# First attention of a two-layer trunk: banks of PSUM given out by use, and TensorE's order written down

## The chip, the cores and the metric

The kernel runs on one core of a Trainium2 chip. The metric is device time in microseconds (us) of one execution. Before the change the median of three runs is 1443.74 us (1443.34 to 1444.59).

## What is computed

A trunk of two layers over 1024 latent tokens (16 rows of 64) and 256 context tokens, model width 1024, 16 heads of 64. Cut to what matters:

```python
u, uc = h * (1 + scale) + shift, hc * (1 + scale_c) + shift_c   # adaLN, per layer
# layer 0, mixer_a: windowed attention, 4 key heads, a sink logit for each head
q, k, v, g = split(u @ w_in);  q, k = apply_axial_rope(q), apply_axial_rope(k)
qc, kc, vc, gc = split(uc @ w_in)
# each block of 128 queries: its own block of keys, one on each side, and the context
p = softmax(concat([mask(q @ k.T), q @ kc.T, sink]))
y = ((p_lat @ v + p_ctx @ vc) * silu(g)) @ w_out     # context queries: context keys only
h = layer_norm(ALPHA * h + gate * y);  hc likewise
# layer 1, mixer_b: 2-D neighbourhood attention with a relative bias, the same frame
```

## The kernel before

Everything is computed as fp32 in two parts, a rounded high part and the rest (`hi`, `lo`), so a product is three matmuls (hi x hi, hi x lo, lo x hi). A program of this size is written with a tile framework: code asks pools for tiles, and a scheduler gives each engine its own list of instructions, in an order that follows from priorities and its own cost estimates. `lift(n)` raises the priority of what stands in it. `keep_in_program_order(ins)` ties an instruction behind the one of its engine that the code issued just before it.

**The stages.** Keys and values of layer 0 are projected first (until 81 us). Then comes the *first attention*, until about 601 us: eight pairs of heads `p`, ten blocks of 128 queries `b` (eight of latents, two of context), two heads `h`; that makes 160 units `A0` to `A159`, twenty a pair. Out-projection and layer norm of layer 0 follow, then layer 1.

**One unit of attention.** Its steps are `S_A` (scores, 256 to 640 keys, matmuls in `qkA`), `m_A` (DVE: scale, mask and minimum out of PSUM into `s`, `sm_first`), the exponential (ACT) with its sum, `rs_A` (DVE), the division (POOL), `T_A` (TensorE transposes of `s` into PSUM, `sm_transpose`), then `pth_A` (ACT: high part of T) and `ptl_A` (DVE: the low part), and for two heads together the value product `pvA` with the high part first and the low part later. `otmp` (ACT and DVE) takes `pvA` out of PSUM.

**Projections between attention.** While pair p is in attention, the g of pair p and the q of pair p+1 are projected: for each, three chunks of tokens (512, 512, 256) named `pj<weights>_<chunk>`, eight pieces of three matmuls a chunk. `merge` weaves the list of attention pieces with the list of projection pieces by their costs. A chunk of q is rotated when it is done (`rope_evac`: shuffle L470 into `rb`, multiply L471 into `ra`, L472 on POOL, add L473), then split into `qA` (L660 on ACT, L661 on DVE). `ra` and `rb` have one buffer each; the third chunk, of context tokens, isn't rotated and goes straight from PSUM into `qA`. A chunk of g goes through `th` (tanh, also in tag `ra`). `gj` and `gw` are dot products for the layer's gate, in between.

**PSUM.** Eight banks: two pairs of banks (`psbig`), which S and T share in turn with whatever else needs a pair, and four single banks (`psone`) for projections and values.

Of the kernel before, what the change touches and what calls it, by code (L numbers as in the profile page):

```python
# [33 lines left out]

AHEAD_A, LIFT_A = 3, 80
AHEAD_B, LIFT_B = 3, 40
BARE_B = 108

GATED_LAST = 1 << 20
# [42 lines left out]

def build(tc, i, out):
    nc = tc.nc
    mm = nc.tensor.matmul
    dma = nc.sync.dma_start
    es = ExitStack()

# [3 lines left out]
        return p, st  # L92

    dr = es.enter_context(tc.tile_pool(name="dr", bufs=1, space=DRAM))
    ps = es.enter_context(tc.tile_pool(name="ps", bufs=1, space=PSUM))

    def psbig(name):
        return ps.tile([P, 1024], F32, tag="big", bufs=2, name=name)

    def psone(name):  # L100
        return ps.tile([P, 512], F32, tag="one", bufs=4, name=name)
# [88 lines left out]
    def proj_pieces(j0, u, chunks, evac):  # L190

        pieces = []
        state = {}

        def piece(ci, t0, n, kq):
            def run():
                if ci == 0 and kq == 0:
                    w.split(j0 + 2)
                    w.split(j0 + 4)
                    w.load(j0 + 6)  # L200
                if kq == 0:
                    state["ps"] = psone(f"pj{j0}_{ci}")
                pt = state["ps"]
                for kt in (kq,):
                    hi, lo = w.got[j0 + kt // 4]
                    sl = slice((kt % 4) * P, (kt % 4 + 1) * P)
                    rh, rl = u.at(kt, slice(t0, t0 + n))
                    mm(pt[:, :n], hi[:, sl], rh, start=kt == 0, stop=False)  # L208
                    mm(pt[:, :n], hi[:, sl], rl, start=False, stop=False)  # L209
                    mm(pt[:, :n], lo[:, sl], rh, start=False, stop=kt == KT - 1)  # L210
# [59 lines left out]

        return evac

    def g_evac(pl, g):


        def evac(pt, t0, n):
            th = pl.tile([P, 512], F32, tag="ra", bufs=1, name="th")
            nc.scalar.activation(th[:, :n], pt[:, :n], AF.Tanh, scale=0.5)
            nc.vector.scalar_tensor_tensor(
                g[:, t0 : t0 + n], th[:, :n], 1.0, pt[:, :n], ALU.add, ALU.mult  # L280
            )

        return evac

    def merge(att, fill, lead=0.0):

        ta = sum(a[0] for a in att) or 1.0
        tf = sum(f[0] for f in fill)
        ia = jf = 0
        ca = cf = 0.0  # L290
# [41 lines left out]
    def sm_transpose(s, order, pt, hl, name):  # L332

        n = len(order)
        tp = psbig(f"T_{name}")
        for k, src in enumerate(order):
            nc.tensor.transpose(tp[:, k * P : (k + 1) * P], s.t[:, src * P : (src + 1) * P], ident)  # L337
        tv = tp[:, : n * P].rearrange("p (k q) -> p k q", k=n)
        a = name[0] == "A"
        with lift(20 if a else 0):  # L340
            nc.scalar.copy(pt.hi[:, :n, hl, :], tv)  # L341
        with lift(60 if a else 0):
            nc.vector.tensor_tensor(pt.lo[:, :n, hl, :], tv, f32(pt.hi[:, :n, hl, :]), ALU.subtract)  # L343
# [116 lines left out]
    adc = pp.tile([P, KT, 2, 2], F32, name="adc")  # L460


    def rope_evac(store, pl, bufs):
        def evac(pt, t0, n):
            if t0 >= S:
                store(pt[:, :n], t0, n)
                return
            a = pl.tile([P, 512], F32, tag="ra", bufs=bufs, name="ra")
            b = pl.tile([P, 512], F32, tag="rb", bufs=bufs, name="rb")
            nc.vector.stream_shuffle(b, pt, SWAP)  # L470
            nc.vector.tensor_tensor(a, pt, cos[:, t0 : t0 + n], ALU.mult)  # L471
            nc.gpsimd.tensor_tensor(b, b, sin[:, t0 : t0 + n], ALU.mult)  # L472
            nc.vector.tensor_tensor(a, a, b, ALU.add)  # L473
            store(a, t0, n)

        return evac
# [125 lines left out]
    def dot_half(h, j):  # L602
        def run():
            dot_sum()
            if j == 0:
                gh.clear()
                for v in range(2):
                    t = px.tile([P, 512], F32, tag=f"gh{v}", bufs=1, name="gh")
                    dma(t, bass.AP(i["cr"].tensor, v * D + h * 512, [[0, P], [1, 512]]))
                    th = px.tile([P, 512], F32, tag="gw", bufs=2, name="gth")  # L610
                    nc.scalar.activation(th, t, AF.Tanh, scale=0.5)
                    nc.vector.scalar_tensor_tensor(t, th, 1.0, t, ALU.add, ALU.mult)
                    gh.append(t)
# [3 lines left out]
            o = ap_.tile([P, 512], F32, tag="ra", bufs=1, name="gj")  # L617
            nc.vector.tensor_tensor_reduce(o, t, gh[0], 0.5, 0.0, ALU.mult, ALU.add, accum_out=acc[:, j, 0:1])
            nc.gpsimd.tensor_tensor(t, t, gh[1], ALU.mult)
            sums.append((t, acc[:, j, 1:2]))  # L620

        return (0.0, run, 0)
# [22 lines left out]
    pp_st.close()  # L645
    pq, pq_st = pool("attA", "right")


    qA, gA, kA, vA = {}, {}, {}, {}

# [12 lines left out]
        return store  # L663

    def qprojA(p):
        return proj_pieces(pos["Aq", p], uA, CHUNKS, rope_evac(q_store(p), ap_, 1))

    def gprojA(p):
        def gev(pt, t0, n):
            if t0 == 0:  # L670
                gA[p] = pq.tile([P, T], F32, tag="gA", bufs=2, name=f"gA{p}")
            g_evac(ap_, gA[p])(pt, t0, n)

        return proj_pieces(pos["Ag", p], uA, CHUNKS, gev)

# [77 lines left out]
    def att_steps(subs, qk, st, tr, pv, last_of_unit, costs, need, ahead, rise, split=False):  # L753
# [3 lines left out]
        for k in range(-ahead, n + 2 + split):  # L757
            row = []

            def t_piece(k=k):  # L760
                if k + 1 < n:
                    with lift(rise(k)):
                        sm_second(st[k + 1])
                if k >= 0:
                    tr(k)

            def s_piece(k=k):
                qk(k + ahead)

            def v_piece(k=k):  # L770
                pv(k - 2)

            def v_first(k=k):
                pv(k - 2, 0)

            def v_second(k=k):
                pv(k - 3, 1)

            if -1 <= k < n:
# [28 lines left out]
    v_loadA(0)  # L808
    merge([], qprojA(0))
    px, px_st = pool("attA2", "right")  # L810
    for p in range(8):
        att = [x for row in rowsA[p * 20 : (p + 1) * 20] for x in row]
        if p % 2 == 0 and p:
            k_load(p // 2, 1)
        if p % 2 == 1 and p < 7:
# [9 lines left out]
        else:  # L825
# [10 lines left out]

            def og_first():
                oA0.extend(og_small(og_load(0, 0)))
                yA0.extend(psone(f"yA0_{nh}") for nh in range(2))

            fill.append((0.0, og_first))
            for n in range(2 * KT):
# [4 lines left out]
                gate_rows(gts[:, v], dcol[:, 0:8, v])  # L847
            raw = og_load(0, 1)
            merge(att[-6:], [])
    px_st.close()  # L850
    pq_st.close()
    ap_st.close()
# [39 lines left out]
    for b in range(10):  # L892
# [24 lines left out]
        if b < 8:  # L917
            dma(zdd[b * P : (b + 1) * P, :], z)
        pend = (b, z)

    def k_evac(dst, pl):
        def evac(pt, t0, n):
# [285 lines left out]
    for b in range(8):  # L1208
# [31 lines left out]
        for sl in parts:  # L1240
            nc.vector.scalar_tensor_tensor(z[:, sl], z[:, sl], rs[:, 1:2], vecs[3][:, sl], ALU.mult, ALU.add)  # L1241
            dma(grid_rows(out, b)[:, :, sl], z[:, sl])
    ob_st.close()
    ub_st.close()
    wp_st.close()
# [94 lines left out]
```

## Time and profile before

| | before |
|---|---|
| median of three runs | 1443.74 us (1443.34 to 1444.59) |
| the profiled execution | 1443.36 us |
| its span in the profile | 1441.6 us |
| granted TensorE clock, mean | 0.994 |
| busy: PE, DVE, ACT, POOL | 97%, 68%, 51%, 44% |

The span runs from the first to the last instruction that the profiler saw; about 1.8 us lie around it. A line of a group gives code line, engine, operation, output and input, shapes and count, then the busy time, the mean ns of one and the idle time of the engine just ahead of it with what ended that. In the timeline the bracket at the end gives the idle time ahead of an instruction and its releaser.

### The profile page before, as it was taken

To read this page: it belongs to the slowest core of one execution; us is meant where nothing else is said; L and a number is where in the kernel's file an instruction comes from. 1 tells how busy PE (TensorE), PEld (TensorE's weight loads), DVE (VectorE), ACT (ScalarE), POOL (GpSimd) and SP (SyncE) were. 2 spreads that over 40 slices of the span, in tenths; PEclk is the share of its full clock that TensorE was granted. 3 is DMA by queue.
4 is the path that set the end of the run, shared out by engine and by line. 5 is a ranking of instruction groups with operands and counts; after the bars stand their busy time and mean duration, and the time that the engine had idled before them with its cause. 6 is when DMAs were issued, how large, how long until landed. Compare 5 with 4: busy or idle time off the path is not lost. (4 is left out here: it accounts for less than half of the span.)

```text
span 1441.6 us, 25151 instructions
## 1 busy us (share of the span) xinstructions
PE 1392.6 (97%) x8816; PEld 1215.4 (84%) x8816; DVE 987.3 (68%) x2216; ACT 733.6 (51%) x1561; POOL 630.8 (44%) x779
## 2 busy tenths in 40 slices
PE   9999999999999999999999999999999999998995
PEld 5887888888888888788898899888988899887775
DVE  4658888878888789566433765555565565667698
ACT  4336776677676778333222545544454444557310
POOL 0326766666666657233211333333233323336664
PEclk9999999999999999999999999999999999999998
DMA  9472114123122114433287565564555565384353
GB/s 367 171 234 81 53 59 132 46 78 97 66 78 63 56 61 128 128 132 132 74 256 217 160 192 159 140 166 145 170 150 156 144 179 146 103 208 145 115 133 93
DMA packets 117229, 195.05 MB, mean 135 GB/s; under 512 B 9328, under 2 KB 57840, under 8 KB 117104
## 3 DMA queue, kind: packets, MB, share of 16 engines
q1 hardware_dynamic: 117104, 193.45, 44.5%
q8 instruction: 70, 1.15, 0.3%
q14 instruction: 55, 0.45, 0.1%
HBM read 141.51 MB, written 51.90 MB: 134 GB/s over the span
## 5 line engine op out<-in xcount | busy, mean ns | idle before, releaser
L330 POOL TENSOR_SCALAR s_B<-s_B,rs_B 128x640 f32<-128x640 f32 (+1 forms) x128 | 101.9, 797 | 292.0 <-DVE rs_B L329 250.9
L208 PE MATMUL pj<-uBh,wh 128*128 128x512 f32 (+1 forms) x448 | 175.9, 393 | 0.0
L209 PE MATMUL pj<-uBl,wh 128*128 128x512 f32 (+1 forms) x448 | 170.2, 380 | 0.0
L210 PE MATMUL pj<-uBh,wl 128*128 128x512 f32 (+1 forms) x448 | 170.0, 379 | 0.0
L325 ACT ACTIVATE s_B<-s_B,m_B 128x640 f32<-128x640 f32 (+1 forms) x128 | 102.9, 804 | 127.9 <-DVE m_B L318 127.7
L325 ACT ACTIVATE s_A<-s_A,m_A 128x641 f32<-128x641 f32 (+2 forms) x160 | 119.5, 747 | 88.5 <-DVE m_A L318 73.5
L164 POOL TENSOR_TENSOR wl<-wr,wh 128x512 fp32r<-128x512 f32 x64 | 87.7, 1371 | 157.8 <-ACT wh L162 135.4
L330 POOL TENSOR_SCALAR s_A<-s_A,rs_A 128x640 f32<-128x640 f32 (+2 forms) x160 | 127.1, 794 | 58.5 <-DVE rs_A L329 56.3
L318 DVE CUSTOM_DVE_ANT_0 s_A<-S_A,msk,nsk 128x640 f32<-128x640 f32 (+2 forms) x160 | 123.6, 774 | 34.0 <-PE S_A L706 17.7
L343 DVE TENSOR_TENSOR pt_B<-T_B,pt_B 128x640 fp32r<-128x640 f32 (+1 forms) x128 | 101.0, 789 | 63.4 <-ACT pt_B L341 62.9
L208 PE MATMUL pj<-uAh,wh 128*128 128x512 f32 (+1 forms) x384 | 139.9, 364 | 0.0
L209 PE MATMUL pj<-uAl,wh 128*128 128x512 f32 (+1 forms) x384 | 137.6, 358 | 0.0
L210 PE MATMUL pj<-uAh,wl 128*128 128x512 f32 (+1 forms) x384 | 137.3, 357 | 0.0
L343 DVE TENSOR_TENSOR ptl_A<-T_A,pth_A 128x640 fp32r<-128x640 f32 (+2 forms) x160 | 114.0, 713 | 15.3 <-PE pvA L734 7.1
L337 PE MATMUL T_A<-ident,s_A 128*128 128x128 f32 x672 | 101.0, 275 | 12.1 <-DVE m_A L318 8.6
L337 PEld LDWEIGHTS T_A<-ident,s_A 128*128 128x128 f32 x672 | 77.2, 140 | 40.2 <-issue 16.6
L341 ACT CAST pt_B<-T_B 128x640 fp32r<-128x640 f32 (+1 forms) x128 | 84.4, 659 | 47.8 <-PE T_B L337 47.4
L318 DVE CUSTOM_DVE_ANT_0 s_B<-S_B,bias 128x640 f32<-128x640 f32 (+1 forms) x128 | 100.5, 785 | 10.6 <-PE S_B L1037 9.6
L341 ACT CAST pth_A<-T_A 128x640 fp32r<-128x640 f32 (+2 forms) x160 | 96.5, 603 | 16.7 <-PE T_A L337 14.0
L210 PEld LDWEIGHTS pj<-uBh,wl 128*128 128x128 f32 x448 | 84.3, 188 | 16.7
L337 PE MATMUL T_B<-ident,s_B 128*128 128x128 f32 x608 | 88.3, 274 | 6.0 <-POOL gB L1078 2.3
L209 PEld LDWEIGHTS pj<-uBl,wh 128*128 128x128 f32 x448 | 84.7, 189 | 9.1
(219 smaller groups left out, 3885.3 us busy)
## 6 DMA issues: line engine op xcount, KB each, us to landing
kB<-kdB SPq DMA_DIRECT2D x64, 320.0 KB, 5.3
gw<-in_wadaT SPq DMA_DIRECT2D x48, 256.0 KB, 2.8
vdB<-st SPq DMA_DIRECT2D x20, 512.0 KB, 3.4
vB<-vdB SPq DMA_DIRECT2D x16, 640.0 KB, 4.8
wada<-in_wadaC SPq DMA_DIRECT2D x16, 512.0 KB, 9.7
kdB<-st SPq DMA_DIRECT2D x16, 512.0 KB, 2.9
qdB<-st SPq DMA_DIRECT2D x16, 512.0 KB, 3.5
qB<-qdB SPq DMA_DIRECT2D x32, 256.0 KB, 4.6
```

The costliest lines, as they stand in the source:

```text
L164: e.tensor_tensor(lo, r, f32(hi), ALU.subtract)
L208: mm(pt[:, :n], hi[:, sl], rh, start=kt == 0, stop=False)
L209: mm(pt[:, :n], hi[:, sl], rl, start=False, stop=False)
L210: mm(pt[:, :n], lo[:, sl], rh, start=False, stop=kt == KT - 1)
L318: nc.vector.tensor_tensor_reduce(outp, sc, in1, scale, init if init is not None else 3e38, ALU.add, ALU.min, accum_out=s.m)
L325: nc.scalar.activation(s.t[:, :n], s.t[:, :n], AF.Exp, bias=s.m, scale=-1.0, accum_out=s.sum)
L330: nc.gpsimd.tensor_scalar(s.t[:, : s.w], s.t[:, : s.w], s.rs, 1.0, ALU.mult, ALU.mult)
L337: nc.tensor.transpose(tp[:, k * P : (k + 1) * P], s.t[:, src * P : (src + 1) * P], ident)
L341: nc.scalar.copy(pt.hi[:, :n, hl, :], tv)
L343: nc.vector.tensor_tensor(pt.lo[:, :n, hl, :], tv, f32(pt.hi[:, :n, hl, :]), ALU.subtract)
```

## The change

1. **Banks by use.** From the end of the key and value projections to the end of the first out-projection block, the pool is a new one: S has one pair of banks, T two pairs in turn, projections one bank (`pj`), value products one bank (`pv`). Before and after that stretch there are pools as before; in the last the pairs take strict turns.
2. **A copy out of the projection bank.** Each chunk of q and g is copied by ACT (L505 of the changed kernel for q, into `ra`; for g into `gA`), with a lift of 40. Shuffle and multiply, tanh and gate then read that copy; the rotation works in `ra` itself. `gj` moves from tag `ra` to `rb`.
3. **A gap behind each chunk.** `merge` holds projection pieces back for 1700 cost units of attention after a chunk's last piece. The hold starts at zero in each call, that is in each pair, and lapses when the attention list is used up.
4. **Values in twos of units.** The value products of an even block are issued high and low part together.
5. **TensorE's order as the code writes it**, for pairs 0 to 6 (`pin`); the eighth pair is left to the scheduler. At the start of every second pair the first three score pieces are moved back by a row or so.

```diff
+LIFT_PJ = 40
+GAP_PJ = 1700.0
...
-    mm = nc.tensor.matmul
+    pinned = []
+    def pin(ins):
+        if pinned:
+            tc.keep_in_program_order(ins)
+    def mm(*a, **kw):
+        pin(nc.tensor.matmul(*a, **kw))
...
+        def big(self, name):
+            use = name[0] if name[0] in self.tags else "S"
+            t = self.tags[use]
+            n = self.n[use] = self.n.get(use, -1) + 1
+            return self.ps.tile([P, 1024], F32, tag=f"big{t[n % len(t)]}", bufs=1, name=name)
+        def one(self, name):
+            if self.ones == 4:
+                return self.ps.tile([P, 512], F32, tag="one", bufs=4, name=name)
+            return self.ps.tile([P, 512], F32, tag=name[:2], bufs=1, name=name)
...
+    banks.st.close()
+    banks.open("psA", {"S": (0,), "T": (1, 2)}, 2)
...
-            return (3 * 0.425 * n, run)
+            return (3 * 0.425 * n, run, GAP_PJ) if kq == 7 and j0 < NA else (3 * 0.425 * n, run)
...
-            if jf < len(fill) and (ia == len(att) or jf < need or cf - lead <= ca * (tf - lead) / ta):
+            if jf < len(fill) and (ia == len(att) or jf < need or (ca >= hold and cf - lead <= ca * (tf - lead) / ta)):
                 cf += fill[jf][0]
                 fill[jf][1]()
+                if len(fill[jf]) > 2:
+                    hold = ca + fill[jf][2]
...
-    def rope_evac(store, pl, bufs):
+    def rope_evac(store, pl, bufs, free=False):
         def evac(pt, t0, n):
+            if t0 < S or free:
+                a = pl.tile([P, 512], F32, tag="ra", bufs=bufs, name="ra")
+            if free:
+                with lift(LIFT_PJ):
+                    nc.scalar.copy(a[:, :n], pt[:, :n])
+                pt = a
...
             if split and 0 <= k - 2 < n and last_of_unit(k - 2):
-                row.append((costs[2] / 2, v_first, 0))
+                if subs[k - 2][1] % 2:
+                    row.append((costs[2] / 2, v_first, 0))
             elif split and k - 3 >= 0 and last_of_unit(k - 3):
-                row.append((costs[2] / 2, v_second, need(k - 3, k + ahead)))
+                if subs[k - 3][1] % 2:
+                    row.append((costs[2] / 2, v_second, need(k - 3, k + ahead)))
+                else:
+                    row.append((costs[2], v_both, need(k - 3, k + ahead)))
...
+        if p == 7:
+            pinned.clear()
+        elif p % 2 == 0 and p:
+            s = [rows_p[n].pop(1) for n in range(3)]
+            rows_p[1].append(s[0])
+            rows_p[2].insert(1, s[1])
+            rows_p[2].append(s[2])
```

**Between two pairs.** TensorE before, at the boundary of pairs 1 and 2 (`pj16_2` is the last chunk of the next pair's q, `pj18_0` the first of that pair's g):

```order
L208 MATMUL pj16_2_2604<-uAh2_107,wh17_1873 128x256
L209 MATMUL pj16_2_2604<-uAl2_110,wh17_1873 128x256
L210 MATMUL pj16_2_2604<-uAh2_107,wl17_1874 128x256
L208 MATMUL pj18_0_2697<-uAh0_105,wh18_2269 128x512
L209 MATMUL pj18_0_2697<-uAl0_108,wh18_2269 128x512
L210 MATMUL pj18_0_2697<-uAh0_105,wl18_2270 128x512
L337 MATMUL T_A37_2703<-ident_63,s_A37_2573 128x128 x2
L705 MATMUL S_A40_2708<-kA1_0_2126,qA4_2426 128x256
```

The same place on TensorE now, where both chunks have the one projection bank:

```order
L96 MATMUL pj16_2_2652<-uAh2_107,wh17_1888 128x256
L96 MATMUL pj16_2_2652<-uAl2_110,wh17_1888 128x256
L96 MATMUL pj16_2_2652<-uAh2_107,wl17_1889 128x256
L96 MATMUL pj18_0_2719<-uAh0_105,wh18_2333 128x512
L96 MATMUL pj18_0_2719<-uAl0_108,wh18_2333 128x512
L96 MATMUL pj18_0_2719<-uAh0_105,wl18_2334 128x512
L372 MATMUL T_A37_2725<-ident_63,s_A37_2586 128x128 x2
```

The chunks still follow each other directly; S_A40 has moved further back. ACT before, at the same place:

```order
L660 CAST qA4_2426<-ra_2583 64x512
L660 CAST qA5_2427<-ra_2583 64x512
L743 COPY otmp_2598<-pvA1_4_2478 64x256
L341 CAST pth_A36_2647<-T_A36_2649 128x2x128
L325 ACTIVATE s_A39_2660,sum_A39_2662<-s_A39_2660,m_A39_2661 128x257
L660 CAST qA4_2426<-pj16_2_2604 64x256
L162 CAST wh21_2689<-wr21_2279 128x512
L341 CAST pth_A36_2647<-T_A37_2703 128x2x128
L660 CAST qA5_2427<-pj16_2_2604 64x256
```

And ACT now; `ra_2596` is the copy of q's second chunk, `ra_2698` that of the third, in the same buffer:

```order
L704 CAST qA4_2445<-ra_2596 64x512
L704 CAST qA5_2446<-ra_2596 64x512
L641 ACTIVATE gw_2485,dcol_71<-gw_2485 128x512
L376 CAST pth_A36_2645<-T_A36_2647 128x2x128
L190 CAST wh21_2711<-wr21_2343 128x512
L505 COPY ra_2698<-pj16_2_2652 128x256
L704 CAST qA4_2445<-ra_2698 64x256
L704 CAST qA5_2446<-ra_2698 64x256
```

The copy of the third chunk stands behind the cast `wh21`; both casts into `qA` come after it.

**At S_A41 and S_A42**, the second and third units of pair 2. TensorE before:

```order
L705 MATMUL S_A41_2745<-kA1_1_2682,qA5_2427 128x256
L706 MATMUL S_A41_2745<-kA1_1_2682,qA5_2427 128x256
L208 MATMUL pj18_0_2697<-uAh0_105,wh19_2273 128x512
L209 MATMUL pj18_0_2697<-uAl0_108,wh19_2273 128x512
L210 MATMUL pj18_0_2697<-uAh0_105,wl19_2274 128x512
L337 MATMUL T_A39_2775<-ident_63,s_A39_2660 128x128 x2
L734 MATMUL pvA1_8_2795<-pth_A36_2647,vA0_981 128x256 x2
L208 MATMUL pj18_0_2697<-uAh0_105,wh19_2273 128x512
L705 MATMUL S_A42_2780<-kA1_0_2126,qA4_2426 128x384
```

TensorE now:

```order
L372 MATMUL T_A39_2782<-ident_63,s_A39_2671 128x128 x2
L96 MATMUL pj18_0_2719<-uAh0_105,wh19_2337 128x512
L96 MATMUL pj18_0_2719<-uAl0_108,wh19_2337 128x512
L96 MATMUL pj18_0_2719<-uAh0_105,wl19_2338 128x512
L96 MATMUL S_A41_2790<-kA1_0_2157,qA5_2446 128x256 x2
L96 MATMUL S_A41_2790<-kA1_1_2704,qA5_2446 128x256 x2
L96 MATMUL S_A42_2802<-kA1_0_2157,qA4_2445 128x384
L96 MATMUL S_A42_2802<-kA1_0_2157,qA4_2445 128x256
```

S_A42 now stands directly behind S_A41, in the one pair of banks that scores have.

**At the start of the first attention.** ACT before, from the evacuation of the last value projection (`pv-1_4`) on:

```order
L266 ACTIVATE st_902<-pv-1_3_853 128x4x64 x2
L266 ACTIVATE st_965<-pv-1_4_908 128x4x64 x2
L660 CAST qA0_1030<-ra_1024 64x512
L660 CAST qA1_1031<-ra_1024 64x512
L162 CAST wh12_1103<-wr12_995 128x512
L162 CAST wh13_1107<-wr13_997 128x512
L660 CAST qA0_1030<-pj8_2_1071 64x256
```

ACT now, where `pj8_0`, `pj8_1` and `pj8_2` are the chunks of the first q:

```order
L294 ACTIVATE st_902<-pv-1_3_853 128x4x64 x2
L294 ACTIVATE st_965<-pv-1_4_908 128x4x64 x2
L505 COPY ra_1028<-pj8_0_1003 128x512
L704 CAST qA0_1035<-ra_1028 64x512
L704 CAST qA1_1036<-ra_1028 64x512
L505 COPY ra_1066<-pj8_1_1041 128x512
L190 CAST wh12_1111<-wr12_999 128x512
```

The copies are new; the first stands behind the evacuation of `pv-1_4`.

More of the change, by code (lines that the diff above doesn't have):

```diff
@@ L94, in build, with open @@
     dr = es.enter_context(tc.tile_pool(name="dr", bufs=1, space=DRAM))
[L95 to L101, printed above, removed]
+    class Banks:
+        def open(self, name, tags, ones):
+            self.st = ExitStack()
+            self.ps = self.st.enter_context(tc.tile_pool(name=name, bufs=1, space=PSUM, reuse_waits="tile"))
+            self.tags, self.ones, self.n = tags, ones, {}
+        def big(self, name):
[7 more added lines that the diff above has]
+            return self.ps.tile([P, 512], F32, tag=name[:2], bufs=1, name=name)
+    banks = Banks()
+    banks.open("ps0", {"S": (0, 1)}, 4)
+    psbig, psone = banks.big, banks.one
     cp = es.enter_context(tc.tile_pool(name="cp", bufs=1, side="left"))
@@ L838, in og_first @@
                 oA0.extend(og_small(og_load(0, 0)))
-                yA0.extend(psone(f"yA0_{nh}") for nh in range(2))
+                banks.tags["T"] = (1,)
+                y = banks.ps.tile([P, 1024], F32, tag="big2", bufs=1, name="yA0")
+                yA0.extend(y[:, sl] for sl in HALVES)
             fill.append((0.0, og_first))
@@ L919, in build @@
         pend = (b, z)
+        if b == 0:
+            banks.st.close()
+            banks.open("psB", {"S": (0, 1)}, 4)
     def k_evac(dst, pl):
```

26 lines of the change are left out of this document (18 added, 8 removed).

## The prediction

> **What bounds the kernel now.** I read the page's engine lines first, then the stretches, then TensorE's waits in the first attention, then single stretches of the timeline.
>
> ```profile
> span 1441.6 us, 25151 instructions
> PE 1392.6 (97%) x8816; PEld 1215.4 (84%) x8816; DVE 987.3 (68%) x2216; ACT 733.6 (51%) x1561; POOL 630.8 (44%) x779
> ```
>
> PE is busy for 97% of the span, so time can come only from PE's idle time. The change touches nothing outside the first attention that PE would notice. That stretch, 81 to 601 us, has these rows, one for each pair of heads after the start (us, then busy of PE, weight load, DVE, ACT, POOL, clock, DMA):
>
> ```profile
> core 0: us, PE busy (x) PEld busy (x) DVE busy (x) ACT busy (x) POOL busy (x), PEclk, DMA share, GB/s
> 98.20:158.70 60.50, 55.00 (x354) 47.63 (x353) 48.46 (x116) 39.94 (x91) 38.04 (x54) 1.00 0.35 98
> 158.70:218.70 60.00, 58.77 (x385) 51.70 (x385) 49.41 (x122) 42.79 (x98) 40.24 (x58) 1.00 0.20 66
> 218.70:280.40 61.70, 59.34 (x384) 51.69 (x384) 50.63 (x122) 42.43 (x98) 40.45 (x57) 1.00 0.29 89
> 280.40:341.40 61.00, 59.05 (x384) 51.88 (x384) 50.47 (x123) 43.37 (x100) 40.36 (x59) 1.00 0.21 69
> 341.40:403.20 61.80, 59.35 (x384) 51.74 (x384) 50.70 (x122) 42.51 (x98) 40.36 (x57) 1.00 0.30 90
> 403.20:462.90 59.70, 58.50 (x384) 51.79 (x384) 49.06 (x121) 42.50 (x98) 40.25 (x59) 1.00 0.20 62
> 462.90:523.60 60.70, 60.23 (x391) 52.87 (x391) 48.40 (x121) 41.46 (x94) 36.86 (x55) 1.00 0.21 67
> 523.60:601.50 77.90, 71.20 (x439) 61.06 (x438) 61.62 (x138) 52.87 (x113) 42.59 (x61) 1.00 0.36 111
> ```
>
> A pair takes some 60 us at the full granted clock, and PE stands still for 0.5 to 2.5 of it (5.5 and 6.7 in the first and the last; 21.9 us in all eight). DVE is at 80% there, ACT at 70%: they are not the bound, but anything that waits for them waits behind a queue. The waits of PE between 98 and 580 us:
>
> ```profile
> PE T_A L337 <- DVE m_A L318: 8.6, 14, 1.6
> PE S_A L705 <- DVE ptl_A L343: 5.1, 7, 1.2
> PE S_A L706 <- DVE ptl_A L343: 1.8, 6, 0.3
> PE T_A L337 <- POOL gw L619: 1.3, 1, 1.3
> PE T_A L337 <- DVE rs_A L329: 0.5, 1, 0.5
> ```
>
> The first three are waits for a pair of banks: scores S and transposes T take turns in the same two pairs, so a T waits until the first softmax step (`m`, L318) has emptied a later unit's scores, and an S waits until `ptl` has emptied a T. Together 15.5 us in 27 waits: what the new division of banks can give back by name.
>
> **What the change gives.** T gets two pairs of its own; between a T and the `ptl` that frees its pair lie now some 5 us of PE work at the median (3.0 before), counted from the order with the PE prices below. These waits go: -15.5 us. S has one pair alone: S(k+1) may start when `m` of S(k) has run, and nothing else.
>
> **What S waits for now.** The price of one such step, from a place where DVE was prompt:
>
> ```profile
> 212.56 0.41 PE L706 MATMUL S_A<-kA,qA 128*128 128x256 f32 x2
> 213.12 0.48 DVE L318 CUSTOM_DVE_ANT_0 s_A<-S_A,msk,nsk 128x256 f32<-128x256 f32 x1
> 217.35 0.08 DVE L318 DVE_READ_ACCUMULATOR2_ANT m_A<- 128x1 f32 x1
> 217.58 0.41 PE L337 MATMUL T_A<-ident,s_A 128*128 128x128 f32 x2 [0.16 <-DVE m_A L318]
> L318 DVE CUSTOM_DVE_ANT_0 s_A<-S_A,msk,nsk 128x640 f32<-128x640 f32 x96 | 84.6, 881 | 25.8 <-POOL s_A L330 11.7 <-PE S_A L706 11.7 <-POOL s_A L323 1.8
> L318 DVE CUSTOM_DVE_ANT_0 s_A<-S_A,msk,nsk 128x512 f32<-128x512 f32 x32 | 23.7, 749 | 6.2 <-PE S_A L706 5.6
> 111.27 0.74 PE L337 MATMUL T_A<-ident,s_A 128*128 128x128 f32 x5 [0.26 <-DVE m_A L318]
> 111.78 0.44 PE L705 MATMUL S_A<-kA,qA 128*128 128x384 f32 x1
> ```
>
> S ends at 212.97, DVE starts 0.15 later; `m` ends at 217.43 and PE starts 0.15 later; so from the end of one S to the next S it takes 0.15 + 0.88 + 0.08 + 0.15 = 1.26 us for 640 keys, 1.13 for 512, 0.86 for 256. In the new order PE has 1.93 us of other work between at the median, which covers it. It doesn't at 23 of 159 places. At S_A1, S_A42, S_A82, S_A122 and S_A157 nothing lies between (the order at S_A42 is shown); at S_A7 and at the six of S_A31 to S_A131 only five transposes, by the last two rows 0.51 us. Five at 0.86 to 1.13, seven at 0.72, the other eleven together 2.8: 13.2 us. The same arithmetic on before's `T_A <- m_A`, with distances from its order, gives 6.6 us where the trace has 8.6, so it errs low; half of 13.2 (several fall behind a stall in which DVE catches up) to 17.2 (13.2 x 8.6 / 6.6) are the ends. I take 13.2, the plain sum.
>
> **What one projection bank costs at the start.** Before, the three chunks of the first q follow each other without a gap, in three banks. Now each waits for the ACT copy of the one ahead, and in ACT's order the first copy stands behind the evacuation of the value projections:
>
> ```profile
> 86.51 0.39 PE L210 MATMUL pj<-uAh,wl 128*128 128x512 f32 x1
> 86.73 0.39 PE L208 MATMUL pj<-uAh,wh 128*128 128x512 f32 x1
> 90.45 0.39 ACT L266 ACTIVATE st<-pv-1_4_908 128x256 fp32r<-128x256 f32 x1 [0.49 <-DVE st L267]
> 92.17 0.28 PE L208 MATMUL pj<-uAh,wh 128*128 128x256 f32 x1
> L278 ACT ACTIVATE th<-pj 128x512 f32<-128x512 f32 x16 | 9.6, 599 | 2.3 <-PE pj L210 2.1
> L472 POOL TENSOR_TENSOR rb<-rb,sin 128x512 f32<-128x512 f32 x14 | 18.0, 1288 | 10.4 <-DVE rb L470 10.4
> L473 DVE TENSOR_TENSOR ra<-ra,rb 128x512 f32<-128x512 f32 x14 | 10.5, 748 | 0.8 <-POOL rb L472 0.7
> L660 ACT CAST qA<-ra 64x512 fp32r<-64x512 f32 x29 | 17.9, 618 | 5.8 <-DVE ra L473 5.4
> ```
>
> Chunk 0 is done at 86.73 (the row there is the next chunk's first). ACT reaches the copy at 90.84; with 0.60 for 128x512 out of PSUM (L278) and the hand-off PE starts chunk 1 at 91.5: 4.75 us lost. Chunk 1 takes 5.44 (86.73 to 92.17), its copy 0.75: 0.75 lost. Chunk 2 takes 2.9, but its copy goes into the same `ra`, the only one, in which chunk 1's rotation runs: shuffle 0.75 (the row of 211.10 below), POOL 1.29, add 0.75, two casts 1.24, last subtract 0.69, five hand-offs of 0.1, then the 256-wide copy 0.37: 5.6 + 0.15, against 2.9, so 2.85 lost. Start: 8.35 us, between 7.0 and 9.5 as the hand-offs are none or double and DVE is late by a piece.
>
> **What it costs between pairs.** GAP_PJ keeps attention work behind each chunk, but the hold starts from zero in each pair's merge: chunk 2 of q is followed at once by chunk 0 of the next g (the order at this place is shown), in the one bank. Before, the same place, between pairs 1 and 2:
>
> ```profile
> 210.59 0.40 PE L210 MATMUL pj<-uAh,wl 128*128 128x512 f32 x1
> 211.10 0.75 DVE L470 STREAM_SHUFFLE rb<-pj 128x512 f32<-128x512 f32 x1
> 215.55 1.36 DVE L661 TENSOR_TENSOR qA<-ra,qA 64x512 fp32r<-64x512 f32 x1 [0.32 <-ACT qA L660]
> 217.47 0.69 DVE L661 TENSOR_TENSOR qA<-ra,qA 64x512 fp32r<-64x512 f32 x1
> 216.45 0.28 PE L210 MATMUL pj<-uAh,wl 128*128 128x256 f32 x1
> 216.57 0.40 PE L208 MATMUL pj<-uAh,wh 128*128 128x512 f32 x1
> 218.31 0.62 ACT L162 CAST wh<-wr 128x512 fp32r<-128x512 f32 x1
> 218.67 0.39 PE L705 MATMUL S_A<-kA,qA 128*128 128x256 f32 x1 [0.68 <-DVE ptl_A L343]
> ```
>
> Chunk 1 of q is done at 210.82, its rotation leaves `ra` at 218.16, 7.34 us later, since DVE does attention work in between; chunk 2 is done at 216.57, 5.75 us after chunk 1. Now chunk 1's copy (0.60) goes ahead of the shuffle, and chunk 2's copy waits for `ra`: 7.34 + 0.60 + 0.05 + 0.37 + 0.15 = 8.5 us after chunk 1, where PE is ready at 5.75: 2.75 us. Five boundaries have this distance; the first has 5.14 (3.35 lost), the last 6.89 (1.6 lost): 18.7 us over seven. Low end: `ra` is free by then; but the copy stands on ACT behind the cast `wh` of L162, which reuses weights that chunk 2 reads last (the row of 218.31: it ran after chunk 2), so 0.62 + 0.37 + 0.2 = 1.2 us stay at six, 7.5 in all. High end: the sixteen DVE instructions that the new order puts from the shuffle on to the last subtract have 7.2 us of work and start 1.5 us after chunk 1, `ra` free at 9.2: 27.5. I take 18.7, nearest to the measured row.
>
> **The other parts.** 48 copies of 0.37 to 0.6 us are 26 us of ACT work, 3 us a pair, in ACT's 30% of free time: nothing on the path but where the bank is waited for, above. The g chunks and q's first find at least 1.48 us of PE work behind them, over twice a copy; nothing. Shuffle and multiply read SBUF instead of PSUM: L473 does so already at 748 ns, no gain. `gj` in `rb` rather than `ra`: nothing. Values in twos: the same matmuls, their bank is written again at least 3 us after its last matmul (1.1 at one place, at the end); nothing. Transposes and score matmuls keep their count, as do DVE, POOL and SP; no DMA moves past another. Layer B runs as before but for 176 of 3955 matmuls that change places among themselves: nothing. Each wait also drains PE: a 128x256 matmul lasts 0.28 and the next starts 0.12 later (216.45 to 216.57), so 0.16 a wait; 33 waits for 27: +1.0.
>
> [...]
>
> **Sum.** -15.5 + 13.2 + 8.35 + 18.7 + 1.0 = +25.8 us. The profiled execution took 1443.4 (span 1441.6 and 1.8 around it), the median is 1443.7: 1469 us. Its own range: 7.5 + 7.0 + 6.6 - 15.5 = +5.6, or 27.5 + 9.5 + 17.2 + 1.0 - 15.5 = +39.7: 1449 to 1483.
>
> **Rivals.**
> *Faster: one stall absorbs the others.* If PE stands at a boundary, DVE and ACT catch up, and the S waits, which need DVE late or a bare distance, fall into time already lost; only floors remain, 7.5 at boundaries and 7.0 at the start. Against it the gain is 15.5, the further 1.8 us of waits in the rows above and up to 4.6 us, the rest of the 21.9: -7.4, 1436. It decides where all new waits together stay under 16 us. For it: the waits before are few and short (27 of 320 units). Against: S_A1, S_A42, S_A82, S_A122 lie bare in the order, and the start's 4.75 us are independent of DVE.
> *No change: boundaries at the floor, S as reckoned at its low half.* 7.5 + 8.35 + 6.6 - 15.5 - 1.8 - 4.6: about 0, 1441 to 1447.
> *Much slower: every group waits.* If ACT is behind by a cast or two when a chunk ends (0.62 each, and 70% busy), a distance of 1.48 to 2.3 us doesn't cover the copy, and some 38 more groups wait 0.4 each: +15 beyond the sum, 1484 or more. Against: the copy's lift of 40 puts it ahead of most in ACT's order.
>
> **Chances.** The forecast 0.68, every group waits 0.09, no change 0.10, faster 0.13. A measurement here tells 0.2%, 2.9 us, from no change. Of the forecast's own mass a little lies above 1483, of the faster case about half below 1439; the range is 1440 to 1484. Faster 0.13, within 0.2% 0.10, slower 0.77.
>
> **What would show it.** In the profile after: `T_A <- m_A` and `S_A <- ptl_A` gone; instead `pj <- ACT ra` with seven waits of 1 to 4 us at the boundaries and three at the start, one over 4 us; `S_A <- m_A` with some 23 waits and 13 us. The stretch from 81 us to the first S longer by 8 us; a middle pair 61 to 64 us. Wrong it would be if ACT's first copy isn't held by the value evacuations, if the rotation leaves `ra` within 6 us, or if pairs get shorter by more than their named waits.

## The result: slower by 5.3%, three times what was forecast

| | before | after |
|---|---|---|
| median | 1444.16 us | 1520.82 us |
| ratio, 95% interval | | 1.053 [1.049, 1.056] |
| profiled execution | 1443.36 us | 1525.82 us (the longest of four; the others 1518.5 to 1521.0) |

The first lines of the page after:

```profile
span 1524.0 us, 25148 instructions
PE 1424.3 (93%) x8815; PEld 1244.7 (82%) x8816; DVE 994.0 (65%) x2216; ACT 758.2 (50%) x1609; POOL 640.0 (42%) x779
PEclk9989999999999999999999999999999999999999
```

The span grew by 82.4 us. PE's idle time (span less busy) went from 49.0 to 99.7, +50.7; its busy time from 1392.6 to 1424.3, +31.7, with the same matmuls. So there are two losses, and the forecast, +25.8, knew only the first. All of the growth lies in the first attention: from its first score matmul to its last transpose 488.1 us before, 559.8 after, and that first matmul came at 110.0 instead of 98.2 us. The granted clock was 0.972 in the profiled execution and 0.980 to 0.981 in the other three, so the profile holds more of the second loss than the median has.

PE's waits between 80 and 680 us, after (us in total, times, longest):

```profile
PE S_A L96 <- DVE m_A L353: 23.7, 23, 3.7
PE pvA L96 <- DVE otmp L788: 21.6, 19, 2.1
PE pj L96 <- ACT ra L505: 18.3, 9, 5.3
PE T_A L372 <- POOL s_A L358: 2.8, 5, 0.9
PE T_A L372 <- DVE rs_A L364: 2.8, 4, 0.7
PE T_A L372 <- DVE ptl_A L378: 2.7, 6, 0.7
PE T_A L372 <- POOL s_A L365: 1.6, 5, 0.7
```

`T_A <- m_A` and `S_A <- ptl_A`, 15.5 us before, are gone, as forecast. In their place stand one wait for each resource that has become single: the scores' pair of banks, the value bank, the projection bank.

**The value bank**, which the prediction put at nothing. The timeline of the boundary of pairs 1 and 2, PE, ACT and DVE:

```profile
234.41 0.75 PE L96 MATMUL pvA<-ptl_A,vA 128*128 128x256 f32 x5
235.73 0.37 ACT L787 COPY otmp<-pvA 64x256 f32<-64x256 f32 x1
237.56 1.13 DVE L512 TENSOR_TENSOR ra<-ra,cos 128x512 f32<-128x512 f32 x1
238.69 0.40 DVE L788 TENSOR_TENSOR otmp<-pvA,otmp 64x256 f32<-64x256 f32 x1
239.12 0.37 ACT L787 COPY otmp<-pvA 64x256 f32<-64x256 f32 x1 [0.56 <-DVE otmp L788]
240.47 0.42 DVE L788 TENSOR_TENSOR otmp<-pvA,otmp 64x256 f32<-64x256 f32 x1
241.03 0.83 PE L96 MATMUL pvA<-pth_A,vA 128*128 128x256 f32 x5 [2.07 <-DVE otmp L788]
244.22 0.50 PE L96 MATMUL pj<-uAh,wh 128*128 128x512 f32 x1 [1.04 <-ACT ra L505]
```

The value product ends at 235.0; copy, add, copy, add, 1.6 us of work, take until 240.89, because both adds stand behind other work in DVE's queue and the second copy waits for the first add. PE reaches the next value product after 4 us and stands 2.07. This stand gives the projection's copy time, so the `pj` wait behind it is 1.04.

**S_A42**, where nothing lies between one score and the next:

```profile
249.87 0.63 PE L96 MATMUL S_A<-kA,qA 128*128 128x256 f32 x4
252.82 0.69 DVE L659 CUSTOM_DVE_ANT_0 gj<-gw,gh 128x512 f32<-128x512 f32 x1 [2.17 <-DMA gw<-in_wadaT]
253.44 0.75 DVE L353 CUSTOM_DVE_ANT_0 s_A<-S_A,msk,nsk 128x512 f32<-128x512 f32 x1
254.25 1.43 PE L96 MATMUL S_A<-kA,qA 128*128 128x384 f32 x4 [3.75 <-DVE m_A L353]
```

`m` of S_A41 stands in DVE's queue behind `gj`, and `gj` waits 2.17 us for a DMA. At most 1.13 us were forecast; it is 3.75. In all, `gj` waits 11.6 us for its DMA between 81 and 700 us, before 1.0.

**The clock.** The stretches around that stand, in order (us, busy of PE, PEld, DVE, ACT, POOL, then the granted clock):

```profile
245.00:249.90 4.90, 4.90 (x32) 4.28 (x31) 4.37 (x10) 2.76 (x9) 3.03 (x4) 1.00 0.53 139
249.90:253.50 3.60, 0.60 (x5) 0.40 (x3) 1.35 (x6) 0.56 (x2) 1.53 (x3) 1.00 0.59 146
253.50:257.00 3.50, 2.75 (x9) 2.35 (x10) 1.66 (x7) 1.00 (x3) 1.37 (x2) 0.50 0.00 0
257.00:260.50 3.50, 3.50 (x15) 3.21 (x14) 0.35 (x2) 0.74 (x2) 1.54 (x3) 0.52 0.00 0
260.50:264.00 3.50, 3.50 (x25) 3.19 (x24) 2.92 (x7) 3.27 (x8) 1.17 (x3) 1.00 0.00 0
```

After 3 us of standing PE ran at half its clock for 7 us: 15 matmuls in 3.5 us where it had 25 later. Between 80 and 720 us the profile after has 14 such places, that of before none. They last 3.4, 6.8 or 10.2 us, 75.1 in all. PE was busy for 65.7 of these; half of that, 32.8, is close to the +31.7.

All 14 begin on one grid of 3.41 us, and in the stretch of this grid ahead of each PE had stood between 1.55 and 3.41 us. How the grid bears on it is seen at one stand, the 2.07 us at the value bank. In the profile after, a line of the grid (239.85) cuts it, and the clock stays up; in that of e11 (below), a run with the same stand, it lies within one stretch, and the clock falls. First after, then e11:

```profile
239.85:243.27 3.42, 2.14 (x16) 1.96 (x16) 3.30 (x7) 2.86 (x8) 3.23 (x5) 1.00 0.96 225
243.27:246.68 3.41, 2.46 (x15) 2.13 (x16) 2.84 (x5) 1.99 (x5) 3.33 (x3) 1.00 0.41 118
```

```profile
239.83:243.24 3.41, 1.33 (x12) 1.21 (x11) 3.32 (x9) 2.66 (x6) 3.22 (x3) 1.00 0.74 182
243.24:246.65 3.41, 2.64 (x12) 2.16 (x11) 2.49 (x4) 2.33 (x7) 3.41 (x4) 0.50 0.69 169
```

The least that PE had stood ahead of one of the 14 is 1.55 us, in the stretch just ahead of 598.3 us. Such a stretch was not always followed by a fall: the clock stayed at 1.00 behind 1.59 us in the stretch from 171.60 us, and in the profile before behind 1.85 us in that from 599.65. What sets the clock on this grid, and where its limit lies, is not shown.

### The profile page after: what moved, and what is told of

Read it like the earlier page. It is cut to its first block, busy times and chain, and to the rows that moved or that the text cites. A ratio compares the mean times of both kernels' runs of the same rounds, so it can differ in the third digit from the quotient of the medians.

```text
span 1524.0 us, 25148 instructions
## 1 busy us (share of the span) xinstructions
PE 1424.3 (93%) x8815; PEld 1244.7 (82%) x8816; DVE 994.0 (65%) x2216; ACT 758.2 (50%) x1609; POOL 640.0 (42%) x779
## 5 line engine op out<-in xcount | busy, mean ns | idle before, releaser
L365 POOL TENSOR_SCALAR s_A<-s_A,rs_A 128x640 f32<-128x640 f32 (+2 forms) x160 | 133.0, 832 | 95.4 <-DVE rs_A L364 92.3
L96 PE MATMUL pj<-uAh,wh 128*128 128x512 f32 (+1 forms) x384 | 149.7, 390 | 18.3 <-ACT ra L505 18.3
L96 PE MATMUL pj<-uAh,wl 128*128 128x512 f32 (+1 forms) x384 | 143.1, 373 | 0.0
L96 PE MATMUL pj<-uAl,wh 128*128 128x512 f32 (+1 forms) x384 | 143.1, 373 | 0.0
L96 PE MATMUL S_A<-kA,qA 128*128 128x384 f32 (+1 forms) x576 | 119.5, 326 | 23.7 <-DVE m_A L353 23.7
L96 PEld LDWEIGHTS S_A<-kA,qA 128*128 128x128 f32 x576 | 91.9, 199 | 35.4 <-DVE m_A L353 31.5
L96 PE MATMUL yA<-woAh,og 128*128 128x512 f32 x320 | 104.1, 399 | 0.0
L372 PEld LDWEIGHTS T_A<-ident,s_A 128*128 128x128 f32 x672 | 81.4, 143 | 27.4 <-POOL s_A L358 9.5
```

The source lines that it names most:

```text
L96: pin(nc.tensor.matmul(*a, **kw))
L365: nc.gpsimd.tensor_scalar(s.t[:, : s.w], s.t[:, : s.w], s.rs, 1.0, ALU.mult, ALU.mult)
L372: pin(nc.tensor.transpose(tp[:, k * P : (k + 1) * P], s.t[:, src * P : (src + 1) * P], ident))
```

## The experiments

Each kernel stands against the kernel before. "PE idle" and "clock lost" are taken from 80 to 720 us of its profile, in stretches of 10 us: the sum of what PE was not busy, and of the length times (1 - granted clock). Both are of one execution each, and the clock differs between executions of one kernel: over the whole span after lost 42.7 us to it in the profiled one and some 30 in the others. So small differences in the last column say nothing.

| kernel | median us | ratio [95%] | PE idle | clock lost |
|---|---|---|---|---|
| before | 1444 | 1 | 21.9 | 0 |
| after | 1520.82 | 1.053 [1.049, 1.056] | 74.5 | 37.6 |
| e1 free order | 1499.24 | 1.038 [1.036, 1.040] | 56.0 | 22.1 |
| e2 strict turns | 1615.75 | 1.119 [1.117, 1.120] | 135.3 | 47.8 |
| e3 lifted evacuation | 1527.26 | 1.058 [1.056, 1.059] | 87.4 | 32.4 |
| e4 idle work, start and scores | 1526.53 | 1.058 [1.055, 1.061] | 72.1 | 27.3 |
| e5 old pool, written order | 1536.57 | 1.064 [1.062, 1.065] | 89.0 | 17.1 |
| e6 old pool, free order | 1484.61 | 1.028 [1.026, 1.029] | 50.8 | 10.3 |
| e7 scores in place | 1513.64 | 1.049 [1.047, 1.051] | 70.0 | 34.0 |
| e8 values as before | 1598.86 | 1.107 [1.105, 1.109] | 128.2 | 61.3 |
| e9 copies alone | 1465.53 | 1.015 [1.013, 1.017] | 37.2 | 3.5 |
| e10 gap and twos alone | 1450.21 | 1.005 [1.003, 1.006] | 20.1 | 0 |
| e11 idle work at scores | 1522.22 | 1.054 [1.052, 1.056] | 68.1 | 23.8 |
| e12 hold kept | 1511.13 | 1.047 [1.044, 1.050] | 71.1 | 20.5 |
| e13 banks alone | 1493.84 | 1.035 [1.032, 1.037] | 50.3 | 13.6 |
| e14 order alone | 1488.83 | 1.030 [1.028, 1.032] | 53.6 | 22.2 |
| e15 copies of g alone | 1441.41 | 0.998 [0.997, 0.999] | 16.7 | 0 |
| e16 twos alone | 1449.20 | 1.003 [1.001, 1.004] | 20.7 | 3.4 |
| e17 copies of g, gap | 1453.91 | 1.007 [1.006, 1.008] | 22.4 | 1.7 |
| e18 copies of q's rotated chunks | 1459.46 | 1.010 [1.009, 1.012] | 33.9 | 0 |

### Banks or order

My theory was that single banks, each held by a chain through DVE's queue, make the waits; the rival, that the written order does. e1 takes away `pinned.append(True)`.

> The changed kernel with TensorE's order left to the scheduler in all pairs (nothing pinned); banks, copies, gap and values as changed. Theory (the waits come from single banks, whoever sets the order): 1505 to 1525 us, S_A on m_A near 20 us and pvA on otmp near 20. Rival (the written order makes PE stand where the scheduler would have gone on): 1460 us or less, both waits under 8.

Between the two, 6 us short of the theory: S_A's wait 12.2 us, pvA's 9.4, `pj`'s 17.6. The written order costs 22 us on top of the rest of the change. e2 was to bring back the old division:

```diff
-    banks.open("psA", {"S": (0,), "T": (1, 2)}, 2)
+    banks.open("psA", {"S": (0, 1)}, 4)
```

> The changed kernel with the old division of PSUM in the first attention (two pairs in strict turns for S and T, four single banks for projections and values); written order, copies, gap and values as changed. Theory (single banks are the cause): waits of pj on ra and of pvA on otmp gone, waits of T_A on m_A and S_A on ptl_A back at 15 to 25 us, 1445 to 1465 us. Rival (the written order or the copies are the cause): 1490 us or more.

It was not the old division. With strict turns of S, T, S, T over two pairs, T has the same one pair each time:

```profile
PE T_A L372 <- DVE ptl_A L378: 97.7, 70, 2.6
PE T_A L372 <- DVE rs_A L364: 15.0, 12, 1.7
```

So it is no test of the banks; it shows what one pair for T costs. e5 and e6 give a pair to whichever tile comes next when one is free, as before; e6 leaves the order free too.

> The changed kernel with PSUM in the first attention divided as before (two pairs given to whichever tile comes next when one is free, four single banks); TensorE's order as written, copies, gap, values in twos as changed. Theory (the single banks make most of the loss, the written order some 20 us): 1455 to 1480 us, pj on ra and pvA on otmp under 5 us together. Rival (a written order needs the changed division, with the old one T and S block each other as in the run with strict turns): 1520 us or more.

> The same old division and the order left to the scheduler: what stays of the change are copies, gap and values in twos. Theory: 1440 to 1455 us, granted clock 1.0 throughout the first attention. Rival (the 48 copies, on ACT ahead of the softmax's steps, cost by themselves): 1465 us or more.

e5 agrees with its rival: with the old division the written order is worse than with the new (`T_A <- m_A` 34.4 us, `S_A <- ptl_A` 20.3). e6, 1485, lies in its rival's range, and its clock did fall (10.3 us lost to it). In both, 8.8 us are a wait of the out-projection at the change of pools that neither before nor after has; without it e5 would be only some 0.5% slower than after. To part the effects, e13 and e14 make one part alone, without copies, gap, twos and moved scores.

> The new division of banks alone: S one pair, T two pairs, one bank for projections, one for values; order free, no copies, no gap, values and scores as before. Theory (one bank each, held by DVE's chains without a copy, is the largest loss): 1500 us or more, pj and pvA waits over 40 us together. Rival (the copies are the larger loss, the division gives back S's and T's waits): 1465 us or less.

> The written order alone: TensorE in program order for pairs 0 to 6, the old division, no copies, no gap, values and scores as before. Theory (the scheduler's order follows when banks come free, a written one doesn't): 1465 to 1500 us, T_A on m_A over 20 us. Rival (the order matters only with copies and gap, which shifted it): 1443 to 1455.

The banks alone cost 3.5%, the order alone 3.0%. In e13 `S_A <- m_A` is 15.2 us, pvA's and pj's waits on DVE together 15.8, not over 40: 1494 is in neither range, near the theory's, and the waits are not where it had them. e14 lies in the theory's range of time, but `T_A <- m_A` is 14.9 us, not over 20; 16.1 us are score matmuls that wait for `kA`'s DMA, which the moved-back scores avoid, and 8.3 the change of pools. Without these two some 19 of its 44 us would be left, an estimate that is near e1's 22. So no single part is the cause: banks, order and copies each cost by themselves, and together less than their sum.

### The value bank

e3 lifts the evacuation: `with lift(LIFT_A):` around the copies and adds into `otmp`.

> The changed kernel with the evacuation of the value products (otmp) lifted by 80, as the first softmax step is. Theory (the value bank is held by an evacuation that stands low in DVE's and ACT's queues): pvA's waits fall from 21.6 to 8 us or less, with the clock loss that follows them 1490 to 1507 us. Rival (DVE is what is short, so the wait only moves to S_A or T_A): 1515 to 1525.

The rival was right that the wait only moves, though not on where, and 1527 is 2 us above its range. pvA's wait fell from 21.6 to 1.2 us and came back elsewhere:

```profile
PE pj L96 <- ACT ra L505: 44.4, 11, 6.6
PE S_A L96 <- DVE m_A L353: 18.4, 17, 1.7
PE T_A L372 <- DVE ptl_A L378: 9.4, 14, 1.2
```

The rotation now holds the projection bank longer. At the boundary of pairs 1 and 2 the `pj` wait is 6.18 us; ahead of it the rotation's add waits 2.40 us for its step on POOL, which started behind other POOL work. The other boundaries were not followed up. e8 undoes the twos:

> The changed kernel with the value products placed as before (high part two units behind, low part three), one value bank. Theory (the one bank and the slow evacuation, about 5 us in DVE's queue, make the wait, not the pairing): pvA on otmp stays at 15 us or more, 1510 to 1535 us. Rival (putting both parts of the even block in one place is what brings pvA too near to the evacuation): pvA under 8 us, 1500 us or less.

The wait rose to 98.0 us: with one value bank the twos are what makes it bearable. The theory was right that the wait stays without the pairing, but 1599 us is far above its range.

### The moved scores, the boundary, the start

e7 leaves out the lines that move three score pieces back; e12 carries the hold over the end of a pair (`hold = carry[0]` at the start of `merge`, `carry[0] = max(0.0, hold - ca)` at its end).

> The changed kernel without the moving back of three score pieces at the start of pairs 2, 4 and 6. Theory (S_A42, S_A82 and S_A122 wait because they stand directly behind the one ahead, and each lets the clock fall): their waits of 3.75, 2.67 and 1.77 us go down to under 1 us, the clock stays up there, 1505 to 1514 us. Rival (the kA load is then waited for instead, which lands some 7 us after its issue): 1519 us or more with S_A on DMA kA of 2 us or more at three places.

> The changed kernel in which the hold behind a chunk is kept over the end of a pair, so that attention work stands between the last chunk of q and the first of the next g. Theory (at the boundary PE waits because the next group follows at once): pj on ra at the seven boundaries from 0.8 to 3.7 us down to 0, so pj in all from 18.3 to 10.5, pvA's 2.07 us ahead of it as they were, 1510 to 1516 us. Rival (the wait moves to the T or S that now come first): 1519 us or more.

e7: the three waits of 3.75, 2.67 and 1.77 us are gone, `S_A <- m_A` is 16.2 us where it was 23.7, and no wait on `kA` is among the larger ones (its 16 loads landed 3.8 to 10.0 us after their issue in the profile after, 5.0 at the median); 1514 us, at the end of the theory's range. Its interval just overlaps that of after, and the clock, 0.979 in three of four executions, is not better than there. e12: `pj`'s wait on its copy went from 18.3 to 7.4 us, two places at the start and the first boundary, and `S_A <- m_A` up to 27.5; 1511, in the theory's range. At the other boundaries the wait was where the order showed it.

### The clock

e4 and e11 put matmuls that compute nothing into unused columns of T's banks, where PE stands.

> The changed kernel with matmuls that compute nothing in three kinds of place where PE stands long: 24 and 28 of them behind the first two steps of the start, 14 ahead of S_A42, S_A82 and S_A122, into unused columns of T's banks. Theory (a long stand of PE lowers its granted clock for the next microseconds, and idle work keeps it up): the waits' ends stay where they are, the granted clock from 85 to 120 us goes from 0.7 to 1.0, 1505 to 1514 us. Rival (the clock falls for another reason, or the stands alone cost): 1520 us or more.

> The changed kernel with 14 matmuls that compute nothing ahead of S_A42, S_A82 and S_A122 alone, in unused columns of T's banks. Theory (PE's standing lowers the granted clock): the second half of 250 to 260 us and the like places at pairs 4 and 6 keep a clock of 1.0 where it was 0.67 to 0.83, 2 to 5 us less in all. Rival (clock and standing have nothing to do with each other): same clock there, no gain.

e4 is no test of the start: its idle matmuls took banks that the evacuation of the value projections still held, and one `pj <- DVE st` wait of 10.0 us took the old one's place. e11 gained nothing in the median. In its profile the three stands are followed by a full clock, so the theory holds there; but the clock fell at 243 us, ahead of the first, where the stand of 2.07 us now lay within one stretch of the grid. Its other three executions had 0.977 to 0.979, no better than after. That the clock falls behind a stand is seen in the profiles, at 14 places in that of after; that filling some of the stands pays was not shown.

### The copies

> The kernel before with the 48 ACT copies out of the projection banks added and nothing else (old banks, free order, no gap, values as before). The prediction's theory (the copies lie beside other work where four single banks are there): 1440 to 1450 us. Rival (they lengthen the rotation's chain and ACT's queue, and the softmax and the T evacuations wait for it): 1455 us or more, S_A on ptl_A above 12 us.

> The kernel before with the gap behind each projection chunk and the values in twos, without copies (old banks, free order). If the copies make the loss that stayed with old banks and free order (1485 us): 1440 to 1450 here. Rival (the gap and the pairs of value products bunch PE's work so that S and T come too near to each other): 1460 us or more with T_A on m_A and S_A on ptl_A above 20 us together.

The copies alone cost 22 us, which the prediction had at nothing. `S_A <- ptl_A` went from 6.9 to 17.9 us, as the rival said: T's low part comes later out of DVE's queue, and the pair of banks with it. Gap and twos cost 7, at the edge of the first range, with T_A's wait on `m_A` down to 3.8 us: less waiting there, more time. These 22 and 7 and the 8.8 at the change of pools are 38 of the 40 us of e6. e15 copies g only; e18 q's two rotated chunks only.

> The kernel before with the copies of g alone (24 of 48). If the loss of the copies alone (22 us) lies in q's longer chain ahead of the attention: 1443 to 1449 us. Rival (each copy costs ACT time ahead of the softmax, q or g): 1452 to 1457.

> The kernel before with q's copies for the two rotated chunks alone (16 of 24), the third straight from PSUM; no copies of g. Theory (DVE's multiply and add take 0.95 and 1.0 us with both inputs in SBUF where they took 0.67 and 0.75, and the chain gets longer by a copy): 1455 to 1465 us, the multiply at 0.9 us or more. Rival (the third chunk's copy into the one ra, which waits for the rotation, makes the 22 us): 1440 to 1449.

g's copies lose nothing, they gain 0.2%, below both ranges; q's rotated chunks alone make 16 of the 22 us, as e18's theory had it. The DVE steps by shape, first before, then e18 (busy, mean ns):

```profile
L661 DVE TENSOR_TENSOR qA<-ra,qA 64x512 fp32r<-64x512 f32 x32 | 27.3, 853 | 4.8 <-ACT qA L660 4.2
L473 DVE TENSOR_TENSOR ra<-ra,rb 128x512 f32<-128x512 f32 x16 | 12.0, 752 | 0.9 <-POOL rb L472 0.7
L471 DVE TENSOR_TENSOR ra<-pj,cos 128x512 f32<-128x512 f32 x16 | 10.8, 673 | 0.0
L470 DVE STREAM_SHUFFLE rb<-pj 128x512 f32<-128x512 f32 x16 | 11.9, 746 | 0.0
```

```profile
L665 DVE TENSOR_TENSOR qA<-ra,qA 64x512 fp32r<-64x512 f32 x32 | 33.0, 1032 | 1.8 <-ACT qA L664 0.9
L477 DVE TENSOR_TENSOR ra<-ra,rb 128x512 f32<-128x512 f32 x16 | 16.4, 1027 | 1.2 <-POOL rb L476 0.7
L475 DVE TENSOR_TENSOR ra<-ra,cos 128x512 f32<-128x512 f32 x16 | 15.5, 968 | 0.0
L474 DVE STREAM_SHUFFLE rb<-ra 128x512 f32<-128x512 f32 x16 | 11.9, 746 | 0.1
```

The multiply went from 673 to 968 ns when its first input moved from PSUM to SBUF; the shuffle, with one input, stayed at 746. The add and the subtract, whose inputs are the same, went up too, from 752 to 1027 and from 853 to 1032. The multiply and POOL's step of the same rotation, a single one of before and then one of e18:

```profile
199.86 1.28 POOL L472 TENSOR_TENSOR rb<-rb,sin 128x512 f32<-128x512 f32 x1 [1.58 <-DVE rb L470]
200.46 0.67 DVE L471 TENSOR_TENSOR ra<-pj,cos 128x512 f32<-128x512 f32 x1
```

```profile
202.64 1.29 POOL L476 TENSOR_TENSOR rb<-rb,sin 128x512 f32<-128x512 f32 x1 [2.01 <-DVE rb L474]
203.23 1.25 DVE L475 TENSOR_TENSOR ra<-ra,cos 128x512 f32<-128x512 f32 x1
```

Both multiplies start 0.6 us into POOL's step; with its input in PSUM DVE needs 0.67 us, with both in SBUF 1.25. Of e18's 16, nine took 0.67 to 0.72 us and seven, each with POOL busy all the while, 1.23 to 1.72; before, all 16 took 0.66 to 0.69. No run changes POOL's work alone, so that POOL makes them longer is not shown.

That the longer steps make the 16 us is not shown. g's DVE step got longer by 0.2 us in e15, and e15 lost nothing (before, then e15):

```profile
L279 DVE SCALAR_TENSOR_TENSOR gA<-th,pj 128x512 f32<-128x512 f32 x16 | 10.8, 678 | 0.0
```

```profile
L282 DVE SCALAR_TENSOR_TENSOR gA<-th,gA 128x512 f32<-128x512 f32 x16 | 14.1, 882 | 2.1 <-ACT th L281 2.1
```

What q's copies have beside it is the copy ahead of a longer chain, and `gj` in `rb`, which the rotation uses too. No run separates these.

> The kernel before with the values in twos alone. With gap and twos T_A's wait on m_A fell from 8.6 to 3.8 us and yet it took 6 us longer. If the gap made the loss and the twos the gain: 1436 to 1443 us. Rival (the twos make the loss): 1447 to 1453.

> The kernel before with the copies of g (which alone gave 0.998) and the gap behind each projection chunk. Theory (the gap spreads the chunks' ends, T_A on m_A fell to 3.8 us with it, and the values in twos made the loss of that run): 1432 to 1440 us. Rival (the gap bunches the projection pieces elsewhere): 1442 to 1450.

Both times the rival's side: the twos alone cost 4 us, and the gap turned g's small gain into a loss of 10 us, 4 us above the rival's range.

**A kernel faster than both:** before with g's copies, e15, 0.998 [0.997, 0.999], a gain of 3.6 us whose interval just leaves out 1. PE's waits there:

```profile
PE S_A L708 <- DVE ptl_A L346: 4.9, 7, 1.1
PE T_A L340 <- DVE m_A L321: 4.0, 8, 1.5
PE S_A L709 <- DVE ptl_A L346: 2.5, 7, 0.7
```

`T_A <- m_A` is 4.0 us where it was 8.6, `S_A <- ptl_A` 7.4 where it was 6.9. Why the copies of g shorten that wait was not tested.

## Why the prediction was right and wrong

The side was right, 1469 forecast; 1521 lies above the range. Three steps failed outright: the one value bank and the copies, both priced at nothing, and PE's busy time, taken as fixed. The waits for the scores' bank were named rightly and mis-sized. Step by step:

- *What the new banks give, 15.5 us:* both waits are gone. But T waits 9.9 us for other things, where it waited 2.2.
- *S on one pair, 13.2 us in 23 places:* 23 waits, 23.7 us, among them all twelve places that were named; the mechanism was right, the size short by 10.5. Its upper end, 17.2, came from prompt chains and one ratio; at S_A42 DVE's queue, with `gj` waiting for a DMA, made 1.13 us into 3.75. S_A42, S_A82 and S_A122 alone took 8.2.
- *The start, 4.75 + 0.75 + 2.85 us:* measured 4.45, 0.68 and 5.30. The last was mis-sized: ACT's order has the gate's `gth` ahead of the casts into `qA`, and it waited for a DMA:

```profile
99.53 0.58 ACT L505 COPY ra<-pj 128x512 f32<-128x512 f32 x1 [3.54 <-PE pj L96]
105.29 0.63 ACT L652 ACTIVATE gth<-gh 128x512 f32<-128x512 f32 x1 [2.90 <-DMA gh<-in_cr]
108.17 0.37 ACT L505 COPY ra<-pj 128x256 f32<-128x256 f32 x1
```

- *Boundaries, 18.7 us:* `pj` waits there 7.9 us, at six of seven; with the 2.07 us that the value bank takes just ahead at five of them it is 18.2. That the sum comes out is luck: more than half of it is a wait that was priced at nothing.
- *"Values in twos: nothing"* failed: the one value bank cost 21.6 us of waits. At least 3 us of PE work between two uses were taken as enough, with no time set against them. The evacuation took 5.9 us through DVE's queue here, for 1.6 us of work, though the same prediction counted queueing for the rotation. That without this wait the kernel would be faster is not shown: e3 took it away and was not.
- *"48 copies: nothing on the path", "no gain" from SBUF* failed: 22 us alone (e9). The 748 ns of the add were read as what two SBUF inputs cost; eight of e18's sixteen took 1.04 to 1.76 us, each with POOL busy beside it. How much of the 22 us lies in that, and how much of them is in the 76.7, stays open.
- *The clock* was not in the sum at all: +31.7 us of busy time. Each stand was priced at its length and 0.16 us, and PE's busy time stood as given. In the first attention of before no single wait is over 1.6 us and the clock never falls there, but the profile before had the price once, in layer 1, where PE stood 2.24 us of 3.41:

```profile
1323.28:1326.69 3.41, 1.17 (x8) 1.00 (x9) 2.29 (x5) 1.77 (x4) 1.99 (x2) 1.00 0.66 233
1326.69:1330.11 3.42, 3.22 (x13) 2.63 (x12) 2.17 (x6) 2.75 (x7) 2.46 (x3) 0.50 0.06 20
```

The stands of 2.75 and 4.75 us that were forecast were the reason to look for it.

- *The rivals:* the S waits did not fall into time already lost, though at the boundaries the value bank's stand took part of `pj`'s; and not every group waited (nine did). What came was a case that none of them named, a stand behind which the next stretch of the grid ran at half clock (14 places).

## To carry to other kernels

When a buffer is made single, compare PE's work between two uses with the latency of the whole chain that frees it, queueing on each engine and waits ahead of it in the queue included, not with the sum of its instructions. A PE stand can have a second price: here, at the 14 places where PE had stood 1.55 to 3.41 us in one stretch of the grid ahead, it was 3.4 to 10.2 us at half clock. 1.59 and 1.85 us in one stretch had no such price, and a stand of 2.07 us had it where it lay within one stretch (e11) but not where the grid cut it (after). Before a PSUM operand is copied to SBUF to free a bank, count the DVE steps that then have two SBUF inputs (here the multiply went from 673 to 968 ns at the mean), and see what POOL does beside them.

## What the runs showed of the hardware

Between 80 and 720 us of the profile after, the granted clock fell to one half 14 times, on one grid of 3.41 us and for one to three stretches of it, each time after a stretch in which PE had stood 1.55 to 3.41 us. Behind 1.59 us in one stretch (after) and 1.85 us (before) it stayed at 1.00. Behind the same stand of 2.07 us it was 0.50 when the stand lay within a stretch (e11) and 1.00 when the grid cut it (after). A DVE multiply of 128x512 took 0.66 to 0.69 us with one input in PSUM (before); with both in SBUF it took 0.67 to 0.72 us nine times and 1.23 to 1.72 us seven times, each of these with POOL busy beside it (e18). A shuffle of 128x512 took 746 ns at the mean, from PSUM (before) as from SBUF (e18).
